# DMA transposes for the feed-forward's product tiles and for most residual pieces of a two-layer encoder

## The chip, the cores and the metric

The kernel runs on one core of one Trainium2 chip. The metric is the device time of one execution in microseconds (us). The kernel before takes 2039.69 us, the median of 3 runs that lie between 2039.32 and 2040.37.

## The reference

A two-layer encoder on 256 tokens of width 2048, in float32. Each layer mixes tokens (layer 0 by a gated mixing within chunks, layer 1 by attention), attends to 256 memory tokens, and ends in a gated feed-forward. Cut to what matters here:

```
for l in range(2):
    h = rms_norm(x, g_mix[l])
    ...                                    # the token mixer and the memory attention, from h
    x = x + concatenate([tok_out, mem_out]) @ w_out[l]
    gate, up = split(rms_norm(x, g_ffn[l]) @ w_gate_up[l], 2)      # 5632 columns each
    x = x + (silu(gate) * up) @ w_down[l]
```

## The kernel before, in words

**Matmuls.** TensorE (PE) needs the activations with features on the partitions, as the stationary operand, and the weights as the moving one, 128 rows by 512 columns. For float32 accuracy every operand is split into a rounded part and a rest (`hi`, `lo`), and a product is three matmuls (`matmul3`, L196 to L200). The weights are split as they arrive: SyncE's queue (SP) loads a raw tile of four 128x512 blocks, ScalarE (ACT) casts it to `whi` (L254), VectorE (DVE) subtracts to `wlo` (L255). There are four raw buffers, and three buffers each of `whi` and `wlo`: ACT can cast a tile only when PE has finished with the buffer's last content.

**Feed-forward.** Tokens lie in two halves (t = 0, 1) of 128. The 5632 features are 11 blocks of 512 (f), in three chunks: f = 0 to 3, 4 to 7, 8 to 10. For each f a `Pair` (L310) computes the gate's and the up's 512 columns for both halves, over eight steps of 256 input features. A step is either an "eight" (eight products, 24 matmuls, one cast of 2048 columns) or, for three of the steps of most blocks, a "seven": seven products of combined weights and activations (21 matmuls, casts of 2048 columns and of a tile T of 1536 columns). Then ACT applies SiLU (L785), DVE multiplies by the up part (L786), and the product tile `sg` (128 tokens x 512 features) is turned: `turn_a` (L764) transposes it on PE in four 128x128 pieces into a PSUM tile `m` (L204), ACT and DVE split that into `hi` and `lo` (L192, L193). For one feature pair of some blocks (`quick`: f = 0, 1, 4, 5 in both layers, and f = 8 in layer 1), ACT also copies half of it (L773), for the sevens of the product with `w_down`. After a chunk, two Pairs multiply its features by `w_down` and add into x.

**Residual pieces.** After `w_out`, and after the last `w_down` chunk of layer 0, x is final in pieces of 128 tokens x 512 columns: `add_residual` (L586) turns a piece on PE (L204), ACT and DVE multiply by the norm's gain and split (L226, L227), and ACT sums its squares (L208).

**What sets the order.** The program puts a turn into a list with a delay counted in matmul steps (`later`, `tick`; 12 steps for most product tiles, 3 for the last block of a chunk). The order on each engine is then fixed when the program is built, by a scheduler. Each engine works through its own queue in order: an instruction that waits holds all behind it.

Of the kernel before, what the change touches and what calls it, by code (L numbers as in the profile page):

```python
# [9 lines left out]

F32 = mybir.dt.float32
F32R = mybir.dt.float32r
AF = mybir.ActivationFunctionType
ALU = mybir.AluOpType
AX = mybir.AxisListType

P = 128
# [10 lines left out]
NB = 512  # L28
# [25 lines left out]
def encoder(ctx: ExitStack, tc: tile.TileContext, x, mem, g_mix, g_ffn, w_in_a, g_v_a, w_spatial, b_spatial,  # L54
            w_in_b, g_q_b, g_k_b, g_mem, w_mem_kv, g_mq, g_mk, w_out, w_gate_up, w_down, rope_c, rope_s, out):
    nc = tc.nc
# [18 lines left out]
    def big(dt=F32, shape=None):  # L75
        return room["p"].tile(shape or [P, NB], dt, tag="a", name=nm("a"))
# [4 lines left out]
    def misc():  # L81
        return psm.tile([P, NB], F32, tag="m", name=nm("m"))

    def v4(a):
        return a.rearrange("p (c n) -> p c n", n=P)
# [34 lines left out]
    X = [[xp.tile([P, NB], F32, name=f"x_{t}_{j}") for j in range(4)] for t in range(NT)]  # L120
# [16 lines left out]
    def gslice(kind, l):  # L137
        return gcol[kind][:, 16 * l:16 * l + 16]

    load_gain("mix", g_mix, kp.tile([32, P], F32, tag="sg", name="gst_mix", bufs=2))  # L140
    nc.scalar.activation(junk[:, :8], mhalf, AF.Square)
    load_x(0, 0)
# [45 lines left out]
    def split(src, shape):  # L188

        hi = big(F32R, shape)  # L190
        lo = big(F32R, shape)
        nc.scalar.copy(hi, src)  # L192
        nc.vector.tensor_tensor(lo, src, hi.bitcast(F32), ALU.subtract)  # L193
        return hi, lo
# [7 lines left out]
    def transpose4(src, dst):  # L202
        for c in range(4):
            nc.tensor.transpose(dst[:, c * P:(c + 1) * P], src[:, c * P:(c + 1) * P], ident)  # L204

    def square_sum(src, out):
        for i in range(2):
            nc.scalar.activation(junk, src[:, 2 * P * i:2 * P * (i + 1)], AF.Square, accum_out=out[:, i:i + 1])  # L208

    def norm_piece(src, t, j, g, parts, keep):  # L210

        tp = misc()
        transpose4(src, tp)
        gained(tp, t, j, g, parts, keep)
        return tp
# [4 lines left out]
    def gained(tp, t, j, g, parts, keep):  # L220

        hi = keep(F32R, [P, 4, P])
        lo = keep(F32R, [P, 4, P])
        for c in range(4):
            gc = g[:, 4 * j + c:4 * j + c + 1]
            nc.scalar.activation(hi[:, c, :], v4(tp)[:, c, :], AF.Copy, scale=gc)  # L226
            nc.vector.scalar_tensor_tensor(lo[:, c, :], v4(tp)[:, c, :], gc, hi[:, c, :].bitcast(F32), ALU.mult,  # L227
                                           ALU.subtract)
            parts.put(4 * j + c, t, hi[:, c, :], lo[:, c, :])
        parts.whole[j, t] = hi, lo  # L230
# [17 lines left out]
    def halves(raw, n, step=KC4):  # L248

        hi = wp.tile([P, KC4, NB], F32R, tag="whi", name=nm("whi"))[:, :n]  # L250
        lo = wp.tile([P, KC4, NB], F32R, tag="wlo", name=nm("wlo"))[:, :n]
        for c in range(0, n, step):
# [37 lines left out]
    def linear(parts, w, n0, units=kd, nk=KD):  # L290
        return Linear(parts, w, n0, nk).run(units)
# [8 lines left out]
    def activation_sums(a0, a1):  # L300

        q = big(F32, [P, 4, P])
        nc.vector.tensor_tensor(q[:, 0], a1[:, 0], a1[:, 1], ALU.subtract)
        nc.vector.tensor_tensor(q[:, 2], a1[:, 0], a0[:, 0], ALU.subtract)
        nc.vector.tensor_tensor(q[:, 1], a0[:, 0], q[:, 0], ALU.subtract)
        nc.vector.tensor_tensor(q[:, 3], a0[:, 1], q[:, 1], ALU.subtract)
        hi, lo = split(q, [P, 4, P])
        return [(hi[:, i, :], lo[:, i, :]) for i in range(4)]
# [106 lines left out]
    def head_norm(acc, r, gain, rope=False):  # L415

        ss = small(8)
        for t in range(NT):
            for h in range(4):
                hs = slice(h * P, (h + 1) * P)  # L420
                nc.scalar.activation(junk[:, :P], acc[t][:, hs], AF.Square, scale=r[t],
                                     accum_out=ss[:, 4 * t + h:4 * t + h + 1])
# [104 lines left out]
    def scaled(acc, r):  # L527

        res = []
        for t in range(NT):  # L530
            hi = big(F32R)
            lo = big(F32R)
            nc.scalar.activation(hi, acc[t], AF.Copy, scale=r[t])
            nc.vector.scalar_tensor_tensor(lo, acc[t], r[t], hi.bitcast(F32), ALU.mult, ALU.subtract)
# [48 lines left out]
            attend(head_norm(acc, r, ghead[f"mq{self.l}"]), (4, 13, 17, 19), lambda: self.kT, lambda: self.V, lambda h: h,  # L583
                   TOK // P, parts)

    def add_residual(acc, j, norm, g, parts):  # L586

        def turn(t):
            norm_piece(X[t][j], t, j, g, parts, kept)
            norm.add(X[t][j], t, j)  # L590
            if j == 3 and t == NT - 1:
                norm.finish()

        for t in range(NT):
            if acc:
                nc.vector.tensor_tensor(X[t][j], acc[t], X[t][j], ALU.add)
            later(1 + t, lambda t=t: turn(t))

    def residual_turns(j, norm, g, parts):
        add_residual(None, j, norm, g, parts)  # L600


    hT = Parts()
    norm = Norm()
    for l in range(DEPTH):
        scope = ExitStack()
        room["p"] = scope.enter_context(tc.tile_pool(name=f"mix{l}", bufs=MIX_TILES, reuse_waits="tile"))
        cat = Parts()
        m = Memory(l)
        if l == 0:  # L610
# [74 lines left out]
            acc = lin.acc  # L685
# [4 lines left out]
            for c in range(3):  # L690
                if c:
                    acc = linear(hT, w, TOK + c * NB)
# [11 lines left out]
            for c in range(3):  # L704
                acc = linear(hT, w, c * NB)
# [5 lines left out]
        else:  # L711
# [4 lines left out]
            acc = linear(hT, w, TOK)  # L716
# [7 lines left out]
            for c in range(3):  # L724
                acc = linear(hT, w, c * NB)
                attend(head_norm(acc, norm.r, ghead["q"], True), (5, 6, 10, 13), lambda: own["k"], lambda: own["v"],
                       lambda h, c=c: (4 * c + h) // 3, 4 * c, cat)
# [4 lines left out]
        hF = Parts()  # L732
        norm = Norm()
        units = kd if l else [(12, KC4), (0, KC4), (4, KC4), (8, KC4)]
        for j in range(4):
            add_residual(linear(cat, w_out[l], j * NB, units), j, norm, gslice("ffn", l), hF)
        room.pop("p")
        scope.close()

# [20 lines left out]
        for chunk in (range(0, 4), range(4, 8), range(8, 11)):  # L760
            aT, aS, half = Parts(), {}, {}
            quick = [2 * f + 1 for f in chunk[:2 if chunk[-1] < 10 else l]]

            def turn_a(a, t, f, aT=aT, aS=aS, half=half, quick=quick):  # L764
                tp = misc()
                transpose4(a, tp)
                hi, lo = split(v4(tp), [P, 4, P])
                for i in range(4):
                    aT.put(4 * f + i, t, hi[:, i, :], lo[:, i, :])
                i = 2 * f + 1  # L770
                if i in quick:
                    half[i, t] = big(F32, [P, 2, P])
                    nc.scalar.copy(half[i, t], v4(tp)[:, 2:4])  # L773
                    if t == NT - 1:
                        aS[i] = activation_sums(half[i, 0], half[i, 1])

            pairs = {}
            for f in chunk:
                order, some = ((3, 4, 5, 0, 6, 1, 7, 2), 2) if f == 0 else ((0, 3, 1, 4, 2, 5, 6, 7), 3)
                pairs[f] = Pair(hF, sums, w_gate_up[l], f * NB, DFF + f * NB, order, fast[:some])  # L780
            for f, g in pairs.items():
                g.run(pairs.get(f + 1))
                for t in range(NT):
                    a = kp.tile([P, NB], F32, tag="sg", name=nm("sg"), bufs=2)
                    nc.scalar.activation(a, g.out[t][0], AF.Silu, scale=norm.r[t])  # L785
                    nc.vector.scalar_tensor_tensor(a, g.out[t][1], norm.r[t], a, ALU.mult, ALU.mult)  # L786
                    later(3 + t if f == chunk[-1] else 12 + t, lambda a=a, t=t, f=f: turn_a(a, t, f))
            last = chunk[-1] == 10
            every = [2 * f + c for f in chunk for c in range(2)]
            slow = [i for i in every if i not in quick]  # L790
            pairs = []
            for jj in range(2):
                order = list(slow)
                for n, i in enumerate(quick):
                    order.insert(2 * n + (0 if jj and not last else 2), i)
                into = [[X[t][2 * jj + n] for n in range(2)] for t in range(NT)]
                pairs.append(Pair(aT, aS, w_down[l], 2 * jj * NB, (2 * jj + 1) * NB, order, quick, into))
            for jj, g in enumerate(pairs):
                g.run(None if jj else pairs[1])
                for j in (2 * jj, 2 * jj + 1):  # L800
                    if last and l < DEPTH - 1:
                        residual_turns(j, next_norm, gslice("mix", l + 1), hT)
                    elif last:
                        for t in range(NT):
                            parts = 2 if j == 3 and t == NT - 1 else 1
                            for i in range(parts):
                                cs = slice(i * NB // parts, (i + 1) * NB // parts)
                                eng = nc.scalar if i else nc.sync
                                eng.dma_start(out[0, t * P:(t + 1) * P, j * NB + cs.start:j * NB + cs.stop],
                                              X[t][j][:, cs])  # L810
        norm = next_norm
# [36 lines left out]
```

## Time and profile before

| | |
|---|---|
| median of 3 runs | 2039.69 us |
| span of the profiled execution, first to last instruction | 2038.5 us |
| PE, DVE, ACT, GpSimd busy | 2027.7, 1605.0, 1095.0, 50.6 us |
| bytes moved by DMA | 396.08 MB, mean 194 GB/s |
| PE transposes in all (L204) | 436, of them 176 of `sg` |

The execution's own time isn't listed beside its span; the median of the runs lies 1.2 us above it. Busy time is a union of intervals, and matmuls overlap by their pipelining, so a busy PE says that its queue didn't stand still, not how quick it was. In a timeline a row is: start, duration, engine, line, operation, output<-input, shapes, count, and in brackets the idle time before it and what ended it.

### The profile page before, as it was taken

The numbers are of one execution on the slowest core, as the hardware profiler recorded it, in microseconds if no ns is written. First come the engines' busy times: TensorE is split into PE (matmuls) and PEld (weight loads), VectorE is DVE, ScalarE is ACT, GpSimd is POOL, SyncE is SP. The second block draws the span as 40 slices with busy tenths as digits, with TensorE's granted clock in tenths as the row PEclk, the third lists the DMA queues.
The fourth block names the chain that finished last, engine by engine and source line by source line (L and its number), as shares of the span: only waits on it lengthen the run. The fifth ranks groups of instructions, "written<-read, shape, count | busy, mean of one in ns | idle before, by whom it ended". The sixth has DMA issues, their size and how long they took to land.

```text
span 2038.5 us, 24693 instructions
## 1 busy us (share of the span) xinstructions
PE 2027.7 (99%) x9298; PEld 1679.9 (82%) x9298; DVE 1605.0 (79%) x1862; ACT 1095.0 (54%) x1389; POOL 50.6 (2%) x80
## 2 busy tenths in 40 slices
PE   9999999999999999999999999999999999999999
PEld 7888888888888888888888888888888888888887
DVE  5675557998879988887566886589979899798876
ACT  7765455454445554444555765555544455444552
POOL 2010000000000000000010100000000000000000
PEclk9999999999999999999999999999999999999999
DMA  9754554646656465665566544555566555565554
GB/s 325 253 179 155 185 188 154 227 165 206 203 190 227 165 207 196 202 227 194 186 198 204 173 133 141 202 185 178 195 206 218 195 184 190 205 221 192 183 197 137
DMA packets 202432, 396.08 MB, mean 194 GB/s; under 512 B 11068, under 2 KB 11432, under 8 KB 202312
## 3 DMA queue, kind: packets, MB, share of 16 engines
q1 hardware_dynamic: 198800, 385.79, 56.6%
q0 software_dynamic: 2048, 6.42, 1.0%
q10 hardware_dynamic: 1464, 2.28, 0.3%
q8 instruction: 73, 1.20, 0.2%
q14 instruction: 47, 0.39, 0.1%
HBM read 390.26 MB, written 4.19 MB: 194 GB/s over the span
## 4 chain that ended last, share of the span: by engine, by line
PE 96%; DVE 3%; DMA 1%; issue 1%; ACT 0%; SPq 0%; DVEq 0%; ACTq 0%
PE acc L200 27%; PE acc L199 27%; PE acc L198 27%; PE m L200 4%; PE m L198 4%; PE m L199 4%; PE m L204 2%; DVE wlo L255 1%; DMA raw<-in_w_gate_up 1%; PE m L500 0%; PE m L643 0%; ACT whi L254 0%; DVE x L413 0%; DVE e L413 0%; DMA x<-in_x 0%
## 5 line engine op out<-in xcount | busy, mean ns | idle before, releaser
L254 ACT CAST whi<-raw 128x2048 fp32r<-128x2048 f32 (+2 forms) x465 | 700.8, 1539 | 585.0 <-PE acc L199 512.5
L255 DVE TENSOR_TENSOR wlo<-raw,whi 128x2048 fp32r<-128x2048 f32 (+2 forms) x465 | 836.4, 1823 | 223.9 <-ACT whi L254 220.1
L198 PE MATMUL acc<-whi,h 128*128 128x512 f32 x1440 | 563.7, 392 | 0.0
L199 PE MATMUL acc<-whi,h 128*128 128x512 f32 x1440 | 562.6, 391 | 0.0
L200 PE MATMUL acc<-wlo,h 128*128 128x512 f32 x1440 | 524.1, 392 | 0.9 <-DVE wlo L255 0.9
L198 PE MATMUL acc<-whi,a 128*128 128x512 f32 x1062 | 414.8, 391 | 0.0
L199 PE MATMUL acc<-whi,a 128*128 128x512 f32 x1062 | 414.2, 390 | 0.0
L200 PE MATMUL acc<-wlo,a 128*128 128x512 f32 x1062 | 398.2, 391 | 0.0
L200 PEld LDWEIGHTS acc<-wlo,h 128*128 128x128 f32 x1440 | 270.6, 188 | 56.6 <-DVE wlo L255 1.5
L199 PEld LDWEIGHTS acc<-whi,h 128*128 128x128 f32 x1440 | 270.7, 188 | 55.3
L198 PEld LDWEIGHTS acc<-whi,h 128*128 128x128 f32 x1440 | 271.0, 188 | 54.0
L200 PEld LDWEIGHTS acc<-wlo,a 128*128 128x128 f32 x1062 | 199.4, 188 | 41.3 <-DVE wlo L255 0.3
L199 PEld LDWEIGHTS acc<-whi,a 128*128 128x128 f32 x1062 | 199.5, 188 | 40.4
L198 PEld LDWEIGHTS acc<-whi,a 128*128 128x128 f32 x1062 | 199.5, 188 | 40.2
L254 ACT CAST whi<-T 128x1536 fp32r<-128x1536 f32 x82 | 121.4, 1480 | 143.8 <-PE acc L199 102.2
L255 DVE TENSOR_TENSOR wlo<-T,whi 128x1536 fp32r<-128x1536 f32 x82 | 143.5, 1750 | 39.1 <-ACT whi L254 39.0
L198 PE MATMUL m<-whi,a 128*128 128x512 f32 x264 | 104.2, 395 | 0.7 <-ACT whi L254 0.7
L199 PE MATMUL m<-whi,a 128*128 128x512 f32 x264 | 102.9, 390 | 0.0
L347 DVE TENSOR_TENSOR raw<-raw 128x512 f32<-128x512 f32 x82 | 56.1, 684 | 54.9 <-DMA raw<-in_w_gate_up 53.5
L200 PE MATMUL m<-wlo,a 128*128 128x512 f32 x264 | 89.6, 389 | 0.0
L192 ACT CAST a<-m 128x512 fp32r<-128x512 f32 x80 | 46.7, 587 | 42.8 <-PE m L204 31.7
L193 DVE TENSOR_TENSOR a<-m,a 128x512 fp32r<-128x512 f32 x80 | 53.8, 682 | 13.1 <-ACT a L192 12.9
(126 smaller groups left out, 1473.1 us busy)
## 6 DMA issues: line engine op xcount, KB each, us to landing
raw<-in_w_gate_up SPq DMA_DIRECT2D x352, 512.0 KB, 4.7
raw<-in_w_down SPq DMA_DIRECT2D x176, 512.0 KB, 5.2
raw<-in_w_out SPq DMA_DIRECT2D x32, 1024.0 KB, 5.1
raw<-in_w_in_a SPq DMA_DIRECT2D x24, 1024.0 KB, 5.2
raw<-in_w_in_b SPq DMA_DIRECT2D x24, 1024.0 KB, 5.1
raw<-in_w_mem_kv SPq DMA_DIRECT2D x16, 1024.0 KB, 5.1
raw<-in_w_in_a SPq DMA_DIRECT2D x7, 512.0 KB, 6.2
x<-in_x SPq DMA_DIRECT2D x8, 256.0 KB, 5.8
```

The lines of the kernel that those rows point to most:

```text
L192: nc.scalar.copy(hi, src)
L193: nc.vector.tensor_tensor(lo, src, hi.bitcast(F32), ALU.subtract)
L198: nc.tensor.matmul(out, lhsT=a[0], rhs=b[0], start=start, stop=False)
L199: nc.tensor.matmul(out, lhsT=a[1], rhs=b[0], start=False, stop=False)
L200: nc.tensor.matmul(out, lhsT=a[0], rhs=b[1], start=False, stop=stop)
L204: nc.tensor.transpose(dst[:, c * P:(c + 1) * P], src[:, c * P:(c + 1) * P], ident)
L254: nc.scalar.copy(hi[:, cut], raw[:, cut])
L255: nc.vector.tensor_tensor(lo[:, cut], raw[:, cut], hi[:, cut].bitcast(F32), ALU.subtract)
L347: nc.vector.tensor_tensor(raw[:, 0], raw[:, 0], raw[:, 1], ALU.add)
```

## The change

A new helper `turned` replaces PE's transposes in two places. It views the float32 tile as pairs of 16-bit words, copies them on ACT into two planes (all low words, all high words, 512 each), has the DMA engines transpose the eight 128x128 blocks of 16-bit words from one SBUF tile into another (issued from ACT's queue), and puts the words together again by a second copy on ACT. What follows, a split or the multiplication by the gain, reads that tile in SBUF instead of a PSUM tile.

```
+    def turned(src):
+
+        a, b = big(F32, [P, 4, P]), big(F32, [P, 4, P])
+        planes = a.bitcast(U16).rearrange("p c n -> p (c n)")
+        nc.scalar.copy(planes.rearrange("p (h n) -> p h n", h=2), src.bitcast(U16).rearrange("p (n h) -> p h n", h=2))
+        nc.scalar.dma_start_transpose(b.bitcast(U16).rearrange("p c n -> p (c n)").rearrange("p (c n) -> p c n", n=P),
+                                      planes)
+        whole = b.bitcast(U16).rearrange("p c n -> p (c n)").rearrange("p (h n) -> p n h", h=2)
+        nc.scalar.copy(planes.rearrange("p (n h) -> p n h", h=2), whole)
+        return a
...
-    def add_residual(acc, j, norm, g, parts):
+    def add_residual(acc, j, norm, g, parts, dma):
 
         def turn(t):
-            norm_piece(X[t][j], t, j, g, parts, kept)
+            if dma:
+                gained(turned(X[t][j]).rearrange("p c n -> p (c n)"), t, j, g, parts, kept)
+            else:
+                norm_piece(X[t][j], t, j, g, parts, kept)
...
-        add_residual(None, j, norm, g, parts)
+        add_residual(None, j, norm, g, parts, j < 2)
...
-            add_residual(linear(cat, w_out[l], j * NB, units), j, norm, gslice("ffn", l), hF)
+            add_residual(linear(cat, w_out[l], j * NB, units), j, norm, gslice("ffn", l), hF, j < 3)
...
             def turn_a(a, t, f, aT=aT, aS=aS, half=half, quick=quick):
-                tp = misc()
-                transpose4(a, tp)
-                hi, lo = split(v4(tp), [P, 4, P])
-                for i in range(4):
-                    aT.put(4 * f + i, t, hi[:, i, :], lo[:, i, :])
+                whole = turned(a)
                 i = 2 * f + 1
                 if i in quick:
                     half[i, t] = big(F32, [P, 2, P])
-                    nc.scalar.copy(half[i, t], v4(tp)[:, 2:4])
+                    nc.scalar.copy(half[i, t], whole[:, 2:4])
                     if t == NT - 1:
                         aS[i] = activation_sums(half[i, 0], half[i, 1])
+                hi, lo = split(whole, [P, 4, P])
+                for i in range(4):
+                    aT.put(4 * f + i, t, hi[:, i, :], lo[:, i, :])
```

All 44 product tiles (11 blocks, two halves, two layers), 12 pieces after `w_out` (the first three columns of pieces, both layers) and 4 pieces after layer 0's last `w_down` chunk take this way. In the changed file the lines are shifted: the first copy is L211, the transfer L212, the second copy L215, the cast of the weights L266 (before L254), SiLU L799, the half copy L784, the split L193, the copy of a PSUM bank L409.

The scheduler places the new work anew. ACT's queue before, in layer 0, where block f=6 begins and `sg_5280`, `sg_5283` are the two halves' products of block f=5 (their turns, `m_5502` first, come after the next casts):

```order
L785 ACTIVATE sg_5280<-e_5138,s_444_2818 128x512
L254 CAST whi_5333<-raw_5286 128x2048
L785 ACTIVATE sg_5283<-e_5139,s_447_2824 128x512
L254 CAST whi_5365<-raw_5325 128x2048
L254 CAST whi_5369<-T_5328 128x1536
L192 CAST a_5224<-a_5219 128x512
L254 CAST whi_5402<-raw_5362 128x2048
L254 CAST whi_5433<-raw_5394 128x2048
L254 CAST whi_5437<-T_5397 128x1536
L254 CAST whi_5474<-raw_5430 128x2048
```

The same place on ACT in the changed program:

```order
L799 ACTIVATE sg_5283<-e_5139,s_453_2824 128x512
L211 COPY a_5502<-sg_5280 128x1024
L266 CAST whi_5365<-raw_5325 128x2048
L266 CAST whi_5369<-T_5328 128x1536
L212 DMA_TRANSPOSE a_5503<-a_5502 128x8x128
L215 COPY a_5502<-a_5503 128x1024
L784 COPY a_5507<-a_5502 128x256
L193 CAST a_5509<-a_5502 128x512
L211 COPY a_5532<-sg_5283 128x1024
L266 CAST whi_5402<-raw_5362 128x2048
L212 DMA_TRANSPOSE a_5533<-a_5532 128x8x128
L266 CAST whi_5433<-raw_5394 128x2048
```

The whole first turn now stands between the casts of `whi_5369` and `whi_5402`, and the copy back follows its transfer directly. One block later (`sg_5604` of f=6), also on ACT, two casts stand between transfer and copy back:

```order
L266 CAST whi_5693<-T_5652 128x1536
L211 COPY a_5826<-sg_5604 128x1024
L212 DMA_TRANSPOSE a_5827<-a_5826 128x8x128
L266 CAST whi_5726<-raw_5686 128x2048
L266 CAST whi_5757<-raw_5718 128x2048
L215 COPY a_5826<-a_5827 128x1024
L266 CAST whi_5761<-T_5721 128x1536
```

Of the 60 transfers, 14 are followed directly by their copy back; behind the others stand casts or other work of ACT. PE's queue loses the transposes; before, they stood among the matmuls like this, in the same block f=6:

```order
L198 MATMUL acc_5355<-whi_5474,h_2626 128x512
L199 MATMUL acc_5355<-whi_5474,h_2627 128x512
L204 MATMUL m_5502<-ident,sg_5280 128x128 x4
L200 MATMUL acc_5313<-wlo_5475,h_2597 128x512
L198 MATMUL acc_5313<-whi_5474,h_2597 128x512
```

And where PE first uses `whi_5402`, its order is the same before and after (here of the changed program):

```order
L201 MATMUL acc_5317<-wlo_5366,a_2879 128x512
L201 MATMUL m_5301<-wlo_5366,a_2879 128x512
L199 MATMUL acc_5313<-whi_5402,h_2597 128x512
L200 MATMUL acc_5313<-whi_5402,h_2598 128x512
L199 MATMUL acc_5317<-whi_5402,h_2597 128x512
L200 MATMUL acc_5317<-whi_5402,h_2598 128x512
L199 MATMUL acc_5355<-whi_5402,h_2626 128x512
```

The last matmuls with `wlo_5366` and the first with `whi_5402` follow each other on PE, so PE stands still there until ACT has cast `whi_5402`. SP's and POOL's queues hold the same transfers in the same order, but for one pair of `w_down` loads that stands two rows elsewhere.

More of the change, by code (lines that the diff above doesn't have):

```diff
@@ L12 @@
 F32R = mybir.dt.float32r
+U16 = mybir.dt.uint16
 AF = mybir.ActivationFunctionType
```

## The prediction

> **What bounds the kernel now.** I read the page first, then the list of waits, then the stretch 656:697 us of layer 0's feed-forward, engine by engine.
>
> ```profile
> span 2038.5 us, 24693 instructions
> PE 2027.7 (99%) x9298; PEld 1679.9 (82%) x9298; DVE 1605.0 (79%) x1862; ACT 1095.0 (54%) x1389; POOL 50.6 (2%) x80
> PEclk9999999999999999999999999999999999999999
> PE 96%; DVE 3%; DMA 1%; issue 1%; ACT 0%; SPq 0%; DVEq 0%; ACTq 0%
> PE acc L200 27%; PE acc L199 27%; PE acc L198 27%; PE m L200 4%; PE m L198 4%; PE m L199 4%; PE m L204 2%; DVE wlo L255 1%; DMA raw<-in_w_gate_up 1%; PE m L500 0%; PE m L643 0%; ACT whi L254 0%; DVE x L413 0%; DVE e L413 0%; DMA x<-in_x 0%
> ```
>
> TensorE is busy nearly all the time at full granted clock, and 96% of the chain of waits is its own: whatever leaves its queue shortens the kernel, unless PE then waits for something else. The transposes (L204) are 2% of that chain, the most that can be had. What else can be late next is seen in the waits and in one stretch of the feed-forward:
>
> ```profile
> ACT whi L254 <- PE acc L199: 614.7, 226, 7.4
> DVE wlo L255 <- ACT whi L254: 259.2, 148, 6.0
> 656.00:697.00 41.00, 41.00 (x185) 33.95 (x184) 36.80 (x39) 22.63 (x19) 0.00 (x0) 1.00 0.61 207
> ```
>
> ScalarE (ACT) waits 615 us for PE to free a `whi` buffer: it has time, but in pieces fixed by PE's progress. In the window (PE, PEld, DVE, ACT, POOL busy) ACT has 22.6 of 41 us, VectorE 36.8. So ACT's total isn't the question; which cast stands behind a wait in ACT's queue is.
>
> **The change: what leaves PE.** The timeline of PE round one group of four transposes, and a pair of groups in the chain:
>
> ```profile
> 444.41 0.40 PE L198 MATMUL acc<-whi,h 128*128 128x512 f32 x1
> 444.64 0.60 PE L204 MATMUL m<-ident,sg 128*128 128x128 f32 x4
> 445.00 0.48 PE L199 MATMUL acc<-whi,h 128*128 128x512 f32 x1
> 445.31 0.63 PE L200 MATMUL acc<-wlo,h 128*128 128x512 f32 x2
> 1002.66 0.87 PE m L204 x8
> 678.34 0.39 PE L198 MATMUL acc<-whi,h 128*128 128x512 f32 x1
> 680.83 0.39 PE L198 MATMUL m<-whi,h 128*128 128x512 f32 x1
> ```
>
> Eleven matmul starts lie between the last two rows' 2.49 us, 0.227 each. From 444.41 to 445.31 stand two matmuls and four transposes: 0.90 - 2 x 0.227 = 0.45, so 0.11 us a transpose; the pair of groups gives 0.87 / 8 = 0.11. The change removes 44 product tiles (11 blocks, 2 token halves, 2 layers) and 12 + 4 residual pieces, 60 x 4 = 240 transposes: **-26.4 us** on PE, all on the path.
>
> **What comes onto ACT.** Each turn adds two copies of 1024 16-bit elements and the issue of a transfer of 256 KB; splits and gain scalings now read SBUF instead of PSUM.
>
> ```profile
> L192 ACT CAST a<-m 128x512 fp32r<-128x512 f32 x80 | 46.7, 587 | 42.8 <-PE m L204 31.7 <-PE m L200 5.3 <-PE m L500 4.7
> L192 ACT CAST a<-a 128x512 fp32r<-128x512 f32 x15 | 9.3, 619 | 1.0 <-DVE a L306 1.0
> L193 DVE TENSOR_TENSOR a<-m,a 128x512 fp32r<-128x512 f32 x80 | 53.8, 682 | 13.1 <-ACT a L192 12.9 <-PE m L199 0.2
> L193 DVE TENSOR_TENSOR a<-a,a 128x512 fp32r<-128x512 f32 x15 | 10.2, 682 | 0.0
> L773 ACT COPY a<-m 128x256 f32<-128x256 f32 x18 | 6.6, 367 | 7.0 <-DVE a L193 7.0
> 668.15 1.92 ACT L254 CAST whi<-raw 128x2048 fp32r<-128x2048 f32 x1 [1.28 <-PE acc L199]
> 669.97 1.49 ACT L254 CAST whi<-T 128x1536 fp32r<-128x1536 f32 x1
> ```
>
> The source costs nothing: 587 against 619 ns on ACT, 682 against 682 on DVE. No row shows a strided 16-bit copy. By the two casts, 0.43 us for 512 elements, 1024 elements take 1.04 us; its bounds are 0.59 (as for 512) and 1.92 (as for 2048), and I take 1.04, element for element. That is 125 us over 60 turns, ACT at some 60%: hidden by its waits for PE, except where the copy stands in front of a cast that PE is about to need.
>
> The transfer itself isn't in the trace. Nearest rows (KB, median us from issue to landing; the last, ns of an issue on ACT's own queue):
>
> ```profile
> memT<-a ACTq DMA_DIRECT2D x8, 256.0 KB, 4.8
> a<-memT POOLq DMA_DIRECT2D x8, 256.0 KB, 3.2
> a<-in_mem POOLq DMA_DIRECT2D x8, 256.0 KB, 8.5
> L562 ACTq DMA_DIRECT2D memT<-a x8: 326/326/366, 59.8 to 118.0; - x8
> ```
>
> Call the landing L. I take 4.8: same size, same queue, and weights moving beside it, as in the feed-forward (DMA share 0.61 above). Bounds are 3.2 and 8.5. [...] Its traffic, 60 x 256 KB beside 396 MB, is small, and the weight loads keep their order on SP, POOL its few transfers: I cost both at nothing, hidden by four raw buffers.
>
> **The wait it adds.** The second copy (L215) waits on ACT for the landing, and everything behind it on ACT waits too. Who waits for that is read at block f=5 of layer 0, in order: "S1" the seven-product unit (casts `whi_5365` and T `whi_5369`), "E4" the eight-product unit after it (`whi_5402`), then `whi_5433`, and E5 (`whi_5474`).
>
> ```profile
> 666.83 0.74 DVE L786 SCALAR_TENSOR_TENSOR sg<-e,s,sg 128x512 f32<-128x512 f32 x1
> 671.35 0.63 ACT L192 CAST a<-a 128x512 fp32r<-128x512 f32 x1
> 675.18 3.73 ACT L254 CAST whi<-raw 128x2048 fp32r<-128x2048 f32 x2 [3.21 <-issue]
> 685.34 3.72 ACT L254 CAST whi<-raw 128x2048 fp32r<-128x2048 f32 x2 [5.05 <-PE acc L199]
> 688.08 0.39 PE L198 MATMUL acc<-whi,h 128*128 128x512 f32 x1
> ```
>
> By the order of PE, E4's first matmul is the row at 678.34, the next unit's first at 680.83 and E5's at 688.08. E4's cast runs from 675.18 to 677.10, so only 1.24 us lie between it and its use; the 3.2 us of idle ACT before it are the whole hole that the new work gets.
>
> Group B (nothing stands between issue and copy back; f=5 of both layers, f=9 of layer 1): the product is there at 667.57, copy to 668.6, S1's casts to 671.9, landing at 671.9 + L, then copy back 1.04, half copy 0.37, split 0.59, second tile's copy 1.04, E4's cast 1.92: ready at 676.9 + L against 678.34. PE waits L - 1.5. At L = 4.8 that is 3.3, twice, and 2.9 without the half copy (f=9): 9.5.
>
> Group A (the T cast, 1.4 us, stands between; f=4 of both layers, layer 0's f=8, f=9, layer 1's f=8): L - 2.9 = 1.9, three times, and 1.5 twice without the half copy: 8.7.
>
> Group C (f=1 of both layers): the issue follows T and a copy, 672.5, and E4's cast follows back, half and split: ready at 676.4 + L, PE waits L - 1.9 = 2.9. The second tile's copy stands ahead of the next unit's cast: 1.82 + 1.04 from cast to cast against 2.49 on PE, 0.4 more. Its own landing then stands before E5: cast of E4 ends 681.2, copy, two casts to 685.4, landing 690.2, back and half 691.6, cast to 693.5, against 688.08 + 3.3: 2.1 more. 5.4 each: 10.8.
>
> The other turns have one to three casts between, or a later one with time. The four last blocks of their chunks show how much:
>
> ```profile
> 496.29 0.71 ACT L785 ACTIVATE sg<-e,s 128x512 f32<-128x512 f32 x1
> 502.64 1.48 ACT L254 CAST whi<-T 128x1536 fp32r<-128x1536 f32 x1 [5.63 <-PE acc L199]
> 509.00 0.39 PE L198 MATMUL acc<-whi,a 128*128 128x512 f32 x1
> ```
>
> Copy after the product at 497.1 to 498.1, landing 502.9, back, split, copy 505.5: the T cast ends 507.0, its first use is 509.00. Nothing, or half a microsecond for the second tile behind it: 4 x 0.5 = 2. The 16 residual pieces lie where every unit has eight products and two units are cast ahead: nothing; without that cover up to 1 us each.
>
> Sum at L = 4.8: 9.5 + 8.7 + 10.8 + 2 = 31.0 lost against 26.4 gained, **+4.6**. Each microsecond of L is worth 12 to 14 us (twelve such waits), zero lies near L = 4.4. Copies at 0.59 or 1.92 move it by about -9 or +18. The span of 2038.5 stands 1.2 below the median 2039.69, and I add the change to the median.
>
> **Rivals.**
> 1. **ACT's wait is mostly covered** (other side): L is near 3.2, as for the SBUF-bound `a<-memT`. Then B pays 4.7, A 0.9, C 4.4, the rest nothing: -26.4 + 10 = -16, 2023.6. For: a transfer within SBUF has no DRAM side. Against: the feed-forward's DMA share of 0.61. It decides from L below about 4.1. With no wait at all 2013.
> 2. **The issue holds ACT**: a transposing issue occupies ACT for longer than the 326 ns of a plain one. Its destination in the order is 128x8x128, eight blocks; if each cost a plain issue, 2.6 us. Midway, 1.5 us, L grows to 6.0 (A 14.7, B 13.1, C 15.6), the cast behind the second issue comes 0.8 late at eight places (6.4), the last blocks pay 2.4: 52 - 26.4 = +26, 2066. Nothing in the trace speaks for or against. [...]
> 3. **The transfer is slow beside the weights**: L = 8.5, as for `a<-in_mem`. A 27, B 21, C 26, last blocks 12, others 4: +63, 2102.
>
> **How the numbers follow.** Forecast (L 4.1 to 5.4) 0.33: at L = 4.8 it gives 2044.3, at 5.0 with the issue at half a microsecond 2047, and I take 2047, since the price of the issue can only add. Rival 1 0.35, rival 2 0.26, rival 3 0.06. A measurement of this kernel can tell about 0.2%, 4.1 us, from no change. Faster: rival 1 and the forecast's low end, 0.38; same 0.12, from the forecast's middle; slower the rest, 0.50. The range runs from 2016 (rival 1 with the cheap copy) to 2086 (rival 2 with the dear copy); rival 3 stays out.
>
> **What would show it.** Right: no L204 on `sg`; ACT idle before L215 by 3 to 4 us where nothing stands between; PE idle released by `whi` casts, about 30 us in all, at the f=5 and f=1 places. Landings of 3 us and no such idle mean rival 1; issues of over a microsecond on ACT's queue, rival 2; landings of 8 us, rival 3. The forecast is wrong if PE loses time elsewhere, such as on weight loads that land late.

## The result, and the profile after

| | before | after |
|---|---|---|
| median of 4 runs each | 2039.83 us | 2049.87 us |
| lowest to highest | 2039.32 to 2040.37 | 2046.25 to 2054.25 |
| span of the profiled execution | 2038.5 | 2048.1 (its time 2049.83) |
| mean granted clock of the runs | 1.000 | 0.993 to 0.996 |

After stands to before as 1.005, 95% interval 1.0036 to 1.0065: slower by 10 us. The forecast was 2047. Its 240 transposes did leave PE, so the new waits, with what follows them, cost some 36 us (10.0 + 26.4), against 31 in the sum at L = 4.8 and some 34 in the forecast of 2047. That they agree is largely chance, as the runs below show: the waits stand in other places than the prediction put them.

The head of the page of after, in the order of the lines shown of before:

```profile
PE 2012.3 (98%) x9058; PEld 1655.7 (81%) x9058; DVE 1605.1 (78%) x1862; ACT 1214.8 (59%) x1509; POOL 50.5 (2%) x80
PEclk9999999999999999999999999999999999999999
PE 88%; DVE 4%; ACT 3%; DMA 3%; issue 1%; SPq 0%; ACTq 0%; DVEq 0%
```

ACT got its 120 us of work and VectorE none. PE was 96% of the chain that ended last and is 88%: VectorE, ACT and the DMA now own pieces of it. The clock digits still read 9, and hide that a short stretch ran at half clock (0.50 from 1801 to 1810 us, in the last section). Next, the prices that the prediction had to bound: the two copies (group view: mean ns of one, then idle before it), and the transfer's line (ns of its issue on ACT's own queue, and the landing):

```profile
L211 ACT COPY a<-sg 128x1024 uint16<-128x1024 uint16 x44 | 45.8, 1042 | 6.3 <-DVE sg L800 6.3
L215 ACT COPY a<-a 128x1024 uint16<-128x1024 uint16 x60 | 70.3, 1172 | 64.1 <-DMA a<-a 64.0
L212 ACTq DMA_TRANSPOSE a<-a x60: 1247/1249/1717, 254.3 to 1990.7; - x60
DMA to landing us min/median/max: 3.1/4.9/9.7
```

The copies take 1.04 and 1.17 us (1.04 taken), the median landing is 4.9 us (4.8 taken). The issue takes 1.25 us, where the sum had at most half a microsecond. And ACT waits 64 us for landings, twice what the sum gave PE to lose. Whether PE loses any of that is another question. Windows of 5 us, at the places of the prediction and at the two places in layer 0 where PE stands longest (columns as in the prediction: PE, PEld, DVE, ACT, POOL busy, clock, DMA share, GB/s):

```profile
420.00:425.00 5.00, 3.01 (x12) 2.18 (x13) 3.43 (x3) 5.00 (x4) 0.00 (x0) 1.00 0.39 66
530.00:535.00 5.00, 2.06 (x7) 1.11 (x8) 3.88 (x8) 1.47 (x1) 0.00 (x0) 1.00 0.45 168
645.00:650.00 5.00, 4.64 (x21) 3.51 (x21) 3.52 (x4) 4.83 (x5) 0.00 (x0) 1.00 0.05 20
785.00:790.00 5.00, 2.95 (x11) 1.49 (x9) 5.00 (x9) 0.35 (x1) 0.00 (x0) 1.00 0.65 210
790.00:795.00 5.00, 3.22 (x12) 2.18 (x13) 2.40 (x3) 1.13 (x1) 0.00 (x0) 1.00 0.00 0
```

Block 1 (first row) loses 2.0 us, not 5.4. Block 4, turned from 625 to 640, costs PE nothing but perhaps the 0.36 us of the row at 645, where 1.9 were forecast, and block 5, turned from 668 to 682, has full windows. But after block 3 (530:535) and after block 7 (785:795), the last blocks of the first two chunks, PE stands still for some 4 us each, and the same happens in layer 1. In before, the windows 785:790 and 790:795 hold 24 matmuls each, without a pause.

**What PE waits for there.** First what PE waits for in the whole run, of the longer waits those that before hardly has (us in total, times, the longest), then PE's waiting rows between 785 and 794 us, and VectorE's row for the second half's `lo` split:

```profile
PE acc L199 <- DVE x L425: 9.3, 8, 2.3
PE m L199 <- ACT whi L266: 6.7, 8, 1.3
PE acc L199 <- ACT whi L266: 4.6, 4, 1.5
```

```profile
787.09 0.50 PE L199 MATMUL acc<-whi,a 128*128 128x512 f32 x1 [1.06 <-DVE x L425]
788.89 0.50 PE L199 MATMUL acc<-whi,a 128*128 128x512 f32 x1 [0.83 <-DVE x L425]
791.18 0.50 PE L199 MATMUL m<-whi,a 128*128 128x512 f32 x1 [1.33 <-ACT whi L266]
792.97 0.73 PE L201 MATMUL m<-wlo,a 128*128 128x512 f32 x2 [0.60 <-DVE wlo L267]
792.83 0.68 DVE L194 TENSOR_TENSOR a<-a,a 128x512 fp32r<-128x512 f32 x1
```

Casts of `whi` release 11.3 us of idle PE in the whole run, where the prediction expected about 30. No row names a transfer. PE waits for accumulators that VectorE's adds into x (L425) free, and for weights cast late. The last row is the clue. In before, the same split (L193) ran at 765.42. Here it runs at 792.83, since it needs a buffer: in the order of the changed program, VectorE's four `lo` splits of the last blocks' second halves wait for PE (`PE_49` is PE's semaphore), where in before none of the feed-forward's splits does:

```
L194 TENSOR_TENSOR a_4162<-a_4156,a_4161 128x512 [waits PE_49]
L194 TENSOR_TENSOR a_6002<-a_5996,a_6001 128x512 [waits PE_49]
L194 TENSOR_TENSOR a_12088<-a_12082,a_12087 128x512 [waits PE_49]
L194 TENSOR_TENSOR a_13928<-a_13922,a_13927 128x512 [waits PE_49]
```

The feed-forward's pool has 26 tiles. `turned` takes two of them for each turn, `a` and `b`, and holds `a` until the split is done. At the end of a chunk, when all of the chunk's splits are alive, the pool is empty: `a_6002` gets the tile of `a_5221`, whose last readers are sevens of the second `w_down` Pair. So the scheduler put PE's last eights of the first Pair for the second half, which need `a_6002`, behind the first seven of the second Pair, and that seven needs accumulators which the first Pair still holds.

This gave three theories. **A**, on record: ACT's wait for the landing holds back the weight casts at blocks 1, 4, 5, 8 and 9. **B**: the pool runs out at blocks 3 and 7. **C**: what A describes happens, but only where nothing covers the landing (block 1, or wherever the scheduler leaves such a place), and each pause of PE costs more than itself, because the granted clock falls behind it (to 0.56 in the window 1800 to 1805 of after).

### The profile page after: what moved, and what is told of

It is laid out like the page before. It is cut to its first block, busy times and chain, and to the rows that moved or that the text cites. A ratio compares the mean times of both kernels' runs of the same rounds, so it can differ in the third digit from the quotient of the medians.

```text
span 2048.1 us, 24306 instructions
## 1 busy us (share of the span) xinstructions
PE 2012.3 (98%) x9058; PEld 1655.7 (81%) x9058; DVE 1605.1 (78%) x1862; ACT 1214.8 (59%) x1509; POOL 50.5 (2%) x80
## 4 chain that ended last, share of the span: by engine, by line
PE 88%; DVE 4%; ACT 3%; DMA 3%; issue 1%; SPq 0%; ACTq 0%; DVEq 0%
PE acc L201 26%; PE acc L200 25%; PE acc L199 25%; PE m L201 4%; PE m L199 4%; PE m L200 3%; DVE wlo L267 2%; ACT whi L266 2%; PE m L205 1%; DMA raw<-in_w_down 1%; DMA raw<-in_w_gate_up 1%; DMA a<-a 1%; PE m L512 0%; DVE x L417 0%; DVE x L425 0%
## 5 line engine op out<-in xcount | busy, mean ns | idle before, releaser
L266 ACT CAST whi<-raw 128x2048 fp32r<-128x2048 f32 (+2 forms) x465 | 701.9, 1538 | 433.0 <-PE acc L200 377.7
L266 ACT CAST whi<-T 128x1536 fp32r<-128x1536 f32 x82 | 121.4, 1480 | 129.8 <-PE acc L200 100.0
L215 ACT COPY a<-a 128x1024 uint16<-128x1024 uint16 x60 | 70.3, 1172 | 64.1 <-DMA a<-a 64.0
L199 PEld LDWEIGHTS m<-whi,a 128*128 128x128 f32 x264 | 49.8, 189 | 18.9 <-ACT whi L266 8.8
```

What stands on the lines that cost most here:

```text
L199: nc.tensor.matmul(out, lhsT=a[0], rhs=b[0], start=start, stop=False)
L215: nc.scalar.copy(planes.rearrange("p (n h) -> p n h", h=2), whole)
L266: nc.scalar.copy(hi[:, cut], raw[:, cut])
```

## The experiments

Times are medians, beside the kernel before on the same chip (2039.7 to 2040.3 us).

**Experiment 1: the copy back goes into the product's own tile.** Theory B undone with every transfer kept: a turn holds one tile of the pool less.

```
-    def turned(src):
+    def turned(src, into=None):
...
-        nc.scalar.copy(planes.rearrange("p (n h) -> p n h", h=2), whole)
-        return a
+        to = a if into is None else into
+        nc.scalar.copy(to.bitcast(U16).rearrange("p c n -> p (c n)").rearrange("p (n h) -> p n h", h=2), whole)
+        return to
...
-                whole = turned(a)
+                whole = turned(a, v4(a))
```

> All 60 transfers stay; the second copy of a product tile writes into the product's own tile (sg) instead of the planes' tile, so that a turn holds one tile of the feed-forward's pool less while its split is made. Theory A (the reckoning on record: the copy back waits for the landing at blocks 1, 4, 5, 8 and 9 and holds the weight casts behind it): nothing changes, 2050 us, within 3. Theory B (the pool of 26 tiles runs out at the last blocks of the first two chunks, 3 and 7: the second half's lo split has to wait for PE, PE's order is turned round and PE then waits for an accumulator bank, some 4 us at four places, with a lower granted clock behind two of them): the four stalls go and PE's order there is that of before, 2029 us, between 2025 and 2034, with blocks 1's stalls of 2 us left.

2046.87 us (12 runs, 2032.45 to 2052.39), ratio 1.0028, interval 1.0015 to 1.0042. On the time, B's number failed. On the place it held: none of the four splits waits for PE any more, and the windows at the four places show no pause like those of after (the longest are 0.5 us at 525 and 1.1 at 1525). Two of them:

```profile
530.00:535.00 5.00, 5.00 (x23) 4.14 (x23) 5.00 (x4) 1.92 (x1) 0.00 (x0) 1.00 0.70 238
785.00:790.00 5.00, 5.00 (x24) 4.14 (x23) 5.00 (x7) 1.49 (x1) 0.00 (x0) 1.00 0.72 238
```

So time was lost somewhere new, and how much differed from run to run by 20 us. Experiment 10 looks for it.

**Experiment 2: the last blocks of the first two chunks turned by PE.**

```
-                whole = turned(a)
+                if f in (3, 7):
+                    tp = misc()
+                    transpose4(a, tp)
+                    whole = v4(tp)
+                else:
+                    whole = turned(a)
```

> Blocks 3 and 7 of both layers, the last of their chunks, are turned by PE as before; the other 52 transfers stay. 32 transposes come back to PE, 32 x 0.11 = 3.5 us. Theory A (the landing waits at blocks 1, 4, 5, 8, 9 cost it all, the last blocks 2 us): 2050 + 3.5 - 2 = 2051 us. Theory B (the last blocks cost four stalls of 4 us and a lower clock behind them, some 20 us): 2050 + 3.5 - 20 = 2033 us, between 2029 and 2037.

2027.71 us, ratio 0.9943, interval 0.9931 to 0.9956. Theory A is out: against the change, 22.2 us are gained although 32 transposes (3.5 us) came back, so the last blocks cost 25.7 us, not 2. In the change's profile PE stands idle at them for 4.3, 3.8, 4.3 and 4.1 us, 16.5 in all; most of the rest is the lower clock behind the two in layer 1 (0.81 and 0.85 in the windows from 1545 to 1555; 0.56, 0.50 and 0.91 from 1800 to 1815).

**Experiment 3: only those blocks by transfer.** As above with `f not in (3, 7)`, and all residual pieces by PE.

> Only blocks 3 and 7 of both layers take the transfer, 8 turns; all other product tiles and all residual pieces are turned by PE as before. 32 transposes leave PE, 3.5 us. Theory A: 2039.8 - 3.5 + 2 = 2038 us. Theory B: 2039.8 - 3.5 + 20 = 2056 us, between 2050 and 2060, so slower by itself than the whole change, with the four stalls of 4 us at the ends of the first two chunks.

2064.53 us, ratio 1.0118, interval 1.0105 to 1.0131: slower by 24.6 than before, by 28.1 counting the 3.5 saved. It is even dearer than B said, and the windows of this run, at block 7 of layer 0, show why:

```profile
790.00:795.00 5.00, 3.59 (x16) 2.63 (x14) 5.00 (x7) 0.00 (x0) 0.00 (x0) 1.00 0.50 165
795.00:800.00 5.00, 2.61 (x6) 1.32 (x6) 3.63 (x7) 1.26 (x1) 0.00 (x0) 0.68 0.40 154
800.00:805.00 5.00, 4.74 (x13) 3.25 (x14) 2.45 (x2) 0.21 (x1) 0.00 (x0) 0.64 0.00 0
```

PE is idle for 1.4 + 2.4 + 0.3 = 4.1 us, and then "busy" with 13 matmuls in 5 us in place of 24, mostly because the clock granted is 0.64. The idle time alone would miss much of the cost: PE's waits for accumulators and `whi` casts in this run are 10.7 and 5.2 us, 16 of the 28.1. Count matmuls, or read the clock's column.

**Experiment 4: only the 16 residual pieces by transfer**, all product tiles by PE.

> Only the 16 residual pieces take the transfer; all product tiles are turned by PE. 64 transposes leave PE, 64 x 0.11 = 7.0 us. Both theories have no stall at these places: 2039.8 - 7 = 2033 us, between 2031 and 2036. If it stays near 2040 the pieces' turns cost about what they save, or a transpose is worth less than 0.11 us; this measures the price of the gain by itself.

2031.02 us, ratio 0.9956, interval 0.9944 to 0.9968: 8.9 us faster. 7.0 were reckoned. The pieces' turns cost nothing, as forecast; the other 1.9 us are not placed. Pauses of PE that before has are at most a small part of them: up to 2000 us, PE's idle time by windows is 6.1 us here and 6.5 in before.

**Experiment 7: only blocks 4, 5, 8 and 9 by transfer** (`f not in (4, 5, 8, 9)` by PE, residual pieces too). This is the reckoning on record by itself: its groups A and B, 18.2 us.

> Only blocks 4, 5, 8 and 9 of both layers take the transfer, with ACT's order there that of the change; all else is turned by PE. 64 transposes leave PE, 7.0 us. The reckoning on record (landing counted from the end of the casts ahead of the transfer: groups A and B, 18.2 us): 2039.8 - 7 + 18.2 = 2051 us. Rival (the transfer goes out while those casts still run, so the landing is over when ACT comes to the copy back, and PE waits at most 0.4 us a block): 2039.8 - 7 + 1 = 2034 us, between 2031 and 2037.

2034.63 us, ratio 0.9974, interval 0.9964 to 0.9984: 5.7 us faster, so 7.0 - 5.7 = 1.3 us of waits and not 18.2. ACT's and its queue's rows at block 5 of layer 0, the very place of the prediction's working:

```profile
667.52 1.05 ACT L211 COPY a<-sg 128x1024 uint16<-128x1024 uint16 x1 [0.52 <-DVE sg L805]
668.47 1.91 ACT L266 CAST whi<-raw 128x2048 fp32r<-128x2048 f32 x1
668.60 1.25 ACTq L212 DMA_TRANSPOSE a<-a  x1
670.29 1.47 ACT L266 CAST whi<-T 128x1536 fp32r<-128x1536 f32 x1
671.67 1.18 ACT L215 COPY a<-a 128x1024 uint16<-128x1024 uint16 x1
```

In the order the transfer stands behind both casts. In the trace its issue begins at 668.60, just behind the end of the copy that it waits for, while the first cast has only started and the second hasn't. The landing runs under the 3.2 us of casts, and the copy back at 671.67 waits for nothing. The prediction counted the landing from 671.9, where the casts end. The landing was also shorter here than its 4.8 us, at most 3.1, but that alone is not the reason: with 4.8 us from 668.60 on, the same sum has the cast ready at 673.6 + 4.8 = 678.4, against 678.34 on PE.

**Experiment 8: only blocks 0 and 1 by transfer**; ACT's order at block 1 is that of the change.

> Only blocks 0 and 1 of both layers take the transfer, with ACT's order at block 1 that of the change (the copy back directly behind the issue, for both halves); all else is turned by PE. 32 transposes leave PE, 3.5 us. The reckoning on record (group C, 5.4 us at each block 1): 2039.8 - 3.5 + 10.8 = 2047 us. By the trace of the change (2 us at each, no lower clock): 2039.8 - 3.5 + 4 = 2040 us; with landings that take 8 us, and the lower clock behind the pause, up to 2047.

2043.26 us, ratio 1.0017, interval 1.0009 to 1.0026: 2.9 us slower, 6.4 us of waits against 10.8 on record. Block 1 of layer 1, ACT's rows and then PE's:

```profile
1425.77 1.25 ACTq L212 DMA_TRANSPOSE a<-a  x1
1431.79 1.16 ACT L215 COPY a<-a 128x1024 uint16<-128x1024 uint16 x1 [6.05 <-DMA a<-a]
```

```profile
1435.76 0.50 PE L199 MATMUL acc<-whi,h 128*128 128x512 f32 x1 [3.14 <-ACT whi L266]
```

Here no cast stands between the two copies, ACT waits 6.0 us, the cast behind them starts only at 1433.81 and PE waits 3.1 us for `whi`. This is the prediction's mechanism in full; group C was the one place for it, and the second half's landing, which the prediction charged with 2.1 more, is hidden like that of block 5.

**Experiment 6: blocks 1, 3 and 7 by PE**, the rest as in the change.

> Blocks 1, 3 and 7 of both layers are turned by PE as before, the other 48 transfers stay, in their place as in the change. 192 transposes leave PE, 21.1 us. Theory B with C (the whole loss lies at blocks 3, 7 and 1): 2039.8 - 21.1 + 2 = 2021 us, between 2018 and 2025. The reckoning on record (blocks 4, 5, 8 and 9 cost 18.2 us): 2039.8 - 21.1 + 18.2 = 2037 us.

2028.83 us, ratio 0.9947, interval 0.9934 to 0.9961: no better than experiment 2, and 8 us above what I expected. The waits of block 1 did not go, they moved to block 2, where the scheduler now leaves one cast behind the issue:

```profile
457.57 1.25 ACTq L212 DMA_TRANSPOSE a<-a  x1
458.99 1.91 ACT L266 CAST whi<-raw 128x2048 fp32r<-128x2048 f32 x1
462.88 1.17 ACT L215 COPY a<-a 128x1024 uint16<-128x1024 uint16 x1 [1.97 <-DMA a<-a]
```

PE waits 1.87 us for the cast that follows at 463.94. Which block is caught is the scheduler's doing; taking blocks away doesn't mend it.

**Experiment 10: the kernel of experiment 1 once more**, for a profile of one of its usual executions.

> The first experiment's kernel once more (copy back into the product's tile, turn in one step), for a profile of an execution of the 2042 to 2052 us that most of its executions took; its first profile was of one that took 2032 us. Theory C: PE stands longer at blocks 1 and 2, because transfers land beside weight loads and later than 5 us, and the granted clock is lower for some 10 us behind each pause; no pause at blocks 3 and 7. Rival: the pauses are the same, and the time goes somewhere else.

2043.09 us, ratio 1.0021, interval 1.0011 to 1.0031, profiled at 2042.80. ACT's and PE's rows at block 1 of layer 0:

```profile
425.60 1.25 ACTq L212 DMA_TRANSPOSE a<-a  x1
434.41 1.16 ACT L216 COPY sg<-a 128x1024 uint16<-128x1024 uint16 x1 [8.85 <-DMA a<-a]
```

```profile
437.42 0.79 PE L199 MATMUL acc<-whi,h 128*128 128x512 f32 x1 [4.98 <-ACT whi L267]
```

```profile
435.00:440.00 5.00, 2.58 (x6) 2.09 (x7) 2.60 (x3) 5.00 (x5) 0.00 (x0) 0.57 0.00 0
```

That is theory C. With the pool mended the scheduler ordered ACT's queue anew, and the second half's transfer of block 1 now stands behind three casts, with its copy back directly behind it. It took 8.8 us to land, ACT stood for all of them, PE for 5.0, and the clock fell to 0.57. The like happens at block 1 of layer 1, where PE waits 2.9 us and the clock falls to 0.77 (1440 to 1445), and at block 2 of layer 1, near 1480. In the first profile of this kernel, of the execution of 2032.45 us, the landing at block 1 of layer 0 was 8.3 us and PE waited 4.4. The place near 1480 is different there. The first row is of this run, the second of the first profile:

```profile
1480.41 1.16 ACT L216 COPY sg<-a 128x1024 uint16<-128x1024 uint16 x1 [4.56 <-DMA a<-a]
1471.38 1.18 ACT L216 COPY sg<-a 128x1024 uint16<-128x1024 uint16 x1 [0.17 <-DMA a<-a]
```

It is the same transfer in the same order, issued at 1472.14 and at 1467.50. It landed after 8.3 us here and after 3.9 us there; here PE stands for 4.15 us and the clock falls, there PE doesn't wait at all.

**Experiment 5: the turn in two steps.** The copy into planes and the issue keep their delay, the copy back and the split come two matmul steps later; the copy back writes into the product's tile as in experiment 1.

```
+                    n = 3 + t if f == chunk[-1] else 12 + t
+                    sent = []
+                    later(n, lambda a=a, sent=sent: sent.extend(planes_out(a)))
+                    later(n + 2, lambda a=a, t=t, f=f, sent=sent: turn_a(a, t, f, sent))
-                    later(3 + t if f == chunk[-1] else 12 + t, lambda a=a, t=t, f=f: turn_a(a, t, f))
```

Here `planes_out` is the first half of `turned`, and `sent` carries its two tiles to the second half.

> All 60 transfers stay. Of a product tile's turn, the first copy and the issue keep their place, the copy back and the split come two matmul steps later, so that two casts of weights stand between issue and copy back at block 1 too, where there was none; and as in the experiment before, the copy back writes into the product's own tile, which keeps the pool large enough. Theory C (what is left in that experiment is ACT standing at block 1 for a landing that takes 3 to 10 us by what the weights move beside it, and the lower clock behind each pause of PE; that also makes its runs differ by 20 us): both go, the sum is 240 x 0.11 = 26.4 us saved with 2 us of other waits, 2016 us, between 2012 and 2021, and the runs lie within 4 us. If the rest has another cause (issues, copies in front of casts, DMA load), it stays between 2032 and 2050.

2012.89 us (2011.61 to 2014.58), ratio 0.9867, interval 0.9854 to 0.9881. It beats before by 27.4 us and the change by 37, with all 60 transfers in it, and its runs lie within 3 us. 27.4 against 26.4 fits the price of a transpose: 0.114 us in place of 0.11, though the 1.9 us of experiment 4 may be among the 27.4. The chain of this run, its waits for landings, and block 1 of layer 0:

```profile
PE 98%; DVE 1%; DMA 1%; ACT 0%; issue 0%; SPq 0%; DVEq 0%
ACT sg L220 <- DMA a<-a: 24.5, 12, 3.4
ACT a L220 <- DMA a<-a: 16.3, 10, 4.1
```

```profile
413.91 1.25 ACTq L212 DMA_TRANSPOSE a<-a  x1
416.28 1.32 ACTq L212 DMA_TRANSPOSE a<-a  x1
419.88 1.17 ACT L220 COPY sg<-a 128x1024 uint16<-128x1024 uint16 x1
```

ACT still waits 41 us for landings, and PE for none of them. Both transfers of block 1 go out before the first copy back, which finds its data there.

**Experiment 9: two steps, but the copy back in the pool's tile again.**

```
-                whole = turned(a, v4(a), sent)
+                whole = turned(a, None, sent)
```

> The two-step turn of the fast version, but the copy back writes into the planes' tile of the feed-forward's pool again, as in the change; ACT's order is that of the two-step version. Theory B (the pool of 26 tiles runs out at blocks 3 and 7, whatever ACT does): the four lo splits that wait for PE are back, with four stalls of 4 us and the lower clock: 2013 + 20 to 28, 2033 to 2041 us. Rival (with the landing's waits gone the pool no longer matters): 2013 us, within 3.

2039.22 us (11 runs), ratio 1.0, interval 0.9991 to 1.0009. One tile for each turn costs 26.3 us, with as many casts between issue and copy back as in experiment 5: the four splits wait for PE again, and behind block 7 of layer 0 PE pauses as in the change, with a lower clock:

```profile
790.00:795.00 5.00, 3.07 (x7) 1.97 (x8) 3.82 (x7) 1.47 (x1) 0.00 (x0) 0.63 0.57 191
```

The four kernels that hold all 60 transfers:

| | turn in one step | turn in two steps |
|---|---|---|
| pool runs out | 2049.9 (the change) | 2039.2 (experiment 9) |
| pool large enough | 2046.9, 2043.1 (experiments 1, 10) | 2012.9 (experiment 5) |

Either cure by itself brings 3 to 11 us, both 37. With the pool short, PE stands at four places; with it mended but the turn in one step, ACT stands for landings at blocks 1 and 2. The two costs don't add. In part that is the scheduler, which lays out ACT's queue anew for each of these programs: in experiment 1 the pool's cure put block 1's second landing where ACT stands 8.8 us for it. A larger pool by itself was not tried.

## Why the prediction was right, and where it was wrong

The time came out within 3 us of the forecast, slower as the likelier side had it. The sum's steps, each by the run that isolates it (a loss is the measured difference plus the transposes that this run saved):

| step of the sum | on record | measured | by |
|---|---|---|---|
| 240 transposes leave PE | -26.4 | -27.4 | experiment 5 |
| groups A and B: blocks 4, 5, 8, 9 | 18.2 | 1.3 | experiment 7 |
| group C: block 1 | 10.8 | 6.4 (with block 0) | experiment 8 |
| last blocks of chunks | 2 | 25.7, 28.1 | experiments 2, 3 |
| residual pieces | 0 | -1.9 | experiment 4 |
| change in all | +7 (+4.6 before the issue) | +10.0 | |

- **What leaves PE: right.** 0.11 us for a transpose, read from two matmul starts around four of them, held to 4% in the sum of 240.
- **What comes onto ACT: right.** Copies of 1.04 and 1.17 us and a landing of 4.9 us at the median, where 4.8 was taken from a plain transfer of the same size. To take these strided 16-bit copies element for element like the casts (1.04 us for 1024) was the right choice between the bounds.
- **The issue: half of rival 2.** It takes 1.25 us on ACT's queue, near that rival's 1.5 and far from the 0.33 of the plain issue in before, but it didn't hold ACT as the rival said: at block 5 a cast of 1.91 us begins at 668.47 and runs under the issue at 668.60.
- **The wait it adds, groups A and B: wrong.** The failed step is "casts to 671.9, landing at 671.9 + L". It reads the order as if the transfer went out when ACT has finished what stands ahead of it. The trace of experiment 7 shows it go out at 668.60, 0.03 us after the copy that it waits for has ended, under the casts. 17 us of the 31 were not there. Rival 1, a short landing, isn't the reason: the median is 4.9 us.
- **Group C: right in kind, too large.** The wait is there, where no cast stands between the two copies; its second half was the same mistake.
- **The last blocks: wrong, and the main cost.** "Nothing, or half a microsecond for the second tile behind it: 4 x 0.5 = 2" asked only when the split could be ready by ACT's and the transfer's times. It didn't ask whether the split had a buffer to write. 26 tiles were counted nowhere in the prediction, though `turned` visibly takes two of them. Experiments 2, 3 and 9 put this at 25 to 28 us.
- **Rival 3** holds for single transfers: the longest landing is 9.7 us in after, and PE loses 5.0 us to one of 8.8 in experiment 10.
- **The forecast's 2047: luck.** Groups A and B were 17 us too dear, group C 4, and the last blocks some 24 too cheap; the errors nearly cancel. By the prediction's own signs its mechanism failed: it named PE losing time elsewhere as the mark of a wrong forecast, and PE loses most at the last blocks; and at f=5, where it expected PE to wait for `whi`, PE doesn't.

The losses measured apart add up to 31.5 to 34 us, and the change lost 36. The rest, 2 to 5 us, isn't placed; blocks 2, 6 and 10 were not tried by themselves. The two profiles of experiment 1's kernel are 10.4 us apart, and some 8 of them are placed: the pause of 4.15 us near 1480, which only the longer execution has, and the clock, which is 0.77 to 0.89 behind 1440 and 1480 there and 1.00 in the other. Why one transfer lands after 3.9 us in one execution and after 8.3 in another stays open, and so does the rest of the 20 us between the runs.

## What to carry to other kernels

Ask of a helper that moves work to another engine not only what it costs there, but what it holds: two more tiles for each turn emptied a pool at a chunk's end, and turned PE's order round at a place where nothing of the moved work is seen. A transfer whose landing takes microseconds (4.7 us at the median in experiment 5) should be issued in one step and picked up in a later one, so that other work stands between: ACT's 41 us of waits for landings cost PE no wait there. And where two such costs overlap, cure both before judging either: each cure alone looked nearly worthless here.

## What the runs showed of the hardware

- **ACT's queue issued a transfer ahead of the casts in front of it**, once what it waited for was there: in experiment 7 at 668.60 us, just behind its copy's end at 668.57, under a cast that began at 668.47 and with another cast still to start (670.29). What stood ahead in the order and only had to be executed didn't delay it. Where a cast ahead still waited, the transfer waited with it: in experiment 6 its copy ends at 456.53, the cast ahead of it waits for PE until 457.55, and the issue is at 457.57. So at these two places "each engine works through its own queue in order" holds for ACT's waits, and not for the end of the work ahead of a transfer.
- **Landings of transfers of the same 256 KB spread from 3.0 us (the shortest in experiment 5) to 9.7 us (the longest in after).** One at block 1 of after took 3.1 us while the DMA engines were two thirds busy; the 8.8 us of experiment 10 ran while they were full (shares of 1.01 to 1.08 between 425.6 and 434.4):

```profile
422.27:425.40 3.13, 2.48 (x12) 1.69 (x11) 2.66 (x2) 3.13 (x3) 0.00 (x0) 1.00 0.66 111
413.00:417.35 4.35, 4.35 (x21) 3.60 (x20) 4.35 (x4) 0.00 (x0) 0.00 (x0) 1.00 1.06 314
```

  The second row, of after too, is a landing of at most 4.35 us at a share of 1.06, so a full share alone doesn't explain 8.8; that stays open.
- **Behind a pause of 2.26 us PE's clock fell to half, for 10.3 us.** After, behind block 7 of layer 1, in windows of 1 us:

```profile
1797.00:1798.00 1.00, 0.70 (x3) 0.30 (x2) 1.00 (x3) 0.00 (x0) 0.00 (x0) 1.00 0.00 0
1798.00:1799.00 1.00, 0.10 (x1) 0.00 (x0) 1.00 (x2) 0.00 (x0) 0.00 (x0) 1.00 0.25 27
1799.00:1800.00 1.00, 0.00 (x0) 0.00 (x0) 1.00 (x3) 0.00 (x0) 0.00 (x0) 1.00 0.98 322
1800.00:1801.00 1.00, 0.64 (x2) 0.56 (x3) 1.00 (x3) 0.00 (x0) 0.00 (x0) 0.82 1.01 375
...
1804.00:1805.00 1.00, 0.05 (x1) 0.05 (x1) 0.07 (x1) 0.90 (x1) 0.00 (x0) 0.50 0.00 0
...
1810.00:1811.00 1.00, 1.00 (x4) 0.73 (x4) 0.00 (x0) 0.00 (x0) 0.00 (x0) 0.56 0.00 0
1811.00:1812.00 1.00, 1.00 (x6) 0.82 (x5) 0.00 (x0) 0.40 (x1) 0.00 (x0) 1.00 0.00 0
```

  The clock falls to 0.50 at about 1800.6 and comes back at 1810.9. Ahead of the fall PE had stood still for 2.26 us up to 1800.36, and for 0.30 shortly before. Of the 10.3 us at half clock PE is busy for some 8.7, so some 4 us of work are lost. In these 10.3 us it stands still again, the last time for 1.13 us up to 1804.95; from there it works without a stop for 5.9 us until the clock is back. Not every pause does this: behind the 3.14 us of experiment 8 above, the windows from 1435 to 1445 read 1.00. Which pauses do is not shown by these runs.
